# The slot table's rows by one indirect DMA of GpSimd per block, and the destination numbers behind the last product on DVE

## The chip, the cores and the metric

One core of a Trainium2 chip runs the whole program. The metric is the time of one execution on the device in microseconds (us), as the median of several runs. PE is TensorE, DVE is VectorE, ACT is ScalarE, POOL is GpSimd and SP is SyncE; SP and ACT can issue hardware DMAs, GpSimd issues DMAs whose descriptors software makes.

## The reference

The kernel computes two layers of a hybrid block over 512 latent tokens and 256 context tokens of 1024 features. In each layer come an adaptive layer norm, one input projection for three parallel mixers (short convolution, windowed attention, chunkwise mLSTM), their merge, and then a mixture of experts in two steps: the best of 4 groups, and in it the best 2 of 8 experts. Only the last concerns the change:

```python
def _hier_moe(h, w_rg, b_rg, w_re, b_re, w_ei, w_eo):
    ...
    g_sel = jnp.argmax(g_logit, axis=-1).astype(jnp.int32)
    ...
    top_l, top_i = lax.top_k(e_logit, TOP_K)
    wts = (jax.nn.softmax(top_l, axis=-1) * g_prob[rows, g_sel][:, None]).reshape(A)
    eid = (g_sel[:, None] * EXPERTS_PER_GROUP + top_i).reshape(A)
    ...
    def expert_block(args):
        xblk, e = args
        gt, up = jnp.split(xblk @ w_ei[e], 2, axis=-1)
        return (jax.nn.silu(gt) * up) @ w_eo[e]
    ...
    out = jax.ops.segment_sum(yb * buf_w[:, None], buf_tok, num_segments=N + 1)
```

An expert's `w_ei` is 1024x1024, its `w_eo` 512x1024, both f32.

## The kernel before, in words

`moe` (from L1186) does the experts of one layer. The weights of the 32 experts are streamed once per layer in 384 chunks of 128x1024 f32, 512 KB each: 8 of `w_ei` and 4 of `w_eo` per expert. SP issues one DMA per chunk (`Chunks.load`, L1223, into the tiles `er`; the tiles `wr`, `wh` and `wl`, which the dense products use too, by `wload`, L300). The chunks go around a ring of 40 tiles and, late in the layer, of 32; `fill` issues them as far as the ring goes, in the order of use that `order` gives.

Which expert comes when is decided at run time: the first NFIX (4) experts are fixed, the others are ranked by their number of tokens (`ranks`, from L1456), so that the k-th place in the program has blocks of a size that suits the k-th rank (`BLOCKS`: one, two or three blocks of 128, 64 or 32 rows). `eid`, a row of 32 integers, holds the expert of every place. SP and ACT read their registers from it.

The slot table `tbl` lies in DRAM, a row of four 32-bit words for each slot of each expert: token, destination row, weight, and one unused. `slots_of(e)` (from L1432) loads the rows of each block of place e into a tile `ib` of 128x4, out of 16 buffers. A block of 128 rows is one ACT DMA; a smaller one repeats itself down the 128 partitions and takes four ACT DMAs of 32x4. The address needs the expert's number, which ACT reads into a register. There are 84 such blocks in both layers, 8 of 128 rows and 76 smaller ones.

One pass of the main loop (from L1500) does expert e: `slots_of(e + 4)`; `fill`; `gather_of(e + 2)`, in which GpSimd gathers the tokens' rows into one of two tiles `xg` (L1268, an indirect DMA by column 0 of `ib`); the last products of `up`; `hidden`, in which PE's sums become `z` or `sg`, are transposed by PE and go through silu (ACT) and a product (DVE) into `g`; `down`, the second product; and `deliver`: ACT scales the sums by column 2 of `ib` into `ys` (L1370), and GpSimd scatters `ys` into `yd` (L1380, an indirect DMA). For blocks under 128 rows the destination rows come from `to`, which DVE computes from column 1 of `ib` (L1372, 128x1, four buffers). Between the halves of `hidden`, PE does the first products of expert e + 1, whose rows it has transposed into `x` (L1320, L1322). `z` is copied by ACT for blocks of 64 rows and by DVE for blocks of 32 (L1353).

Each engine works through its instructions in the order in which the scheduler put them. Every hardware DMA of SP or ACT gets one of eight completion semaphores (DMAHW0 to 7), in turn over both engines, and waits for the one before it on the same semaphore; those of GpSimd use eight others (DMASW0 to 7) in the same way.

Of the kernel before, what the change touches and what calls it, by code (L numbers as in the profile page):

```python
# [12 lines left out]
I32 = mybir.dt.int32  # L13
# [7 lines left out]
DEPTH = 2  # L21
# [7 lines left out]
NE = 32  # L29
# [60 lines left out]
def shape_consts():  # L90
    p = np.arange(128)[:, None]
    j = np.arange(128)[None, :]
    ident = (p == j).astype(np.float32)
    neg = np.float32(-BIG)
    m_prev = np.where(j >= p, 0, neg).astype(np.float32)
    m_next = np.where(j <= p, 0, neg).astype(np.float32)
    l_f = np.where(p <= j, 0, BIG).astype(np.float32)
    l_b = np.where(p >= j, 0, BIG).astype(np.float32)
    tri = 32.0 * (p < j).astype(np.float32)
    ones = np.ones((128, 128), np.float32)  # L100
    pos = np.arange(NL)
    nf = 16
    inv = (np.float32(10000.0) ** (-np.arange(nf, dtype=np.float32) / np.float32(nf))).astype(np.float32)
    cos = np.zeros((128, NL), np.float32)
    sin = np.zeros((128, NL), np.float32)
    for q in range(128):
        d = q % 64
        ps = (pos // 64 if d < 32 else pos % 64).astype(np.float32)
        ang = (ps * inv[d % 16]).astype(np.float32)
        cos[q] = np.cos(ang)  # L110
        sin[q] = np.sin(ang) * (-1.0 if d % 32 < 16 else 1.0)
    rst = np.ones((128, NL), np.float32)
    rst[:32, 0::128] = 0
    rst[32:, 127::128] = 0
    iota = np.broadcast_to(np.arange(32), (128, 32))
    lvl, lvl2 = (np.broadcast_to(np.arange(6) * v, (128, 6)) for v in (4096, 8))
    pidx = np.arange(128)[:, None]
    part = np.concatenate([pidx // 64, pidx // 32], 1)
    tie = np.broadcast_to(np.where(np.arange(32) < NFIX, -1e5 * (1 + np.arange(32)), 0) + 31 - np.arange(32), (128, 32))
    srank = np.broadcast_to(np.array(SRANK).reshape(1, -1), (128, 32 * DEPTH))  # L120
    caps = np.broadcast_to(np.array([sum(b) for bl in BLOCKS for b in bl])[None], (128, 32 * DEPTH))
    slot0 = np.broadcast_to(32 * np.arange(128)[None], (128, 128))
    parts = [("ident", ident), ("mp", m_prev), ("mn", m_next), ("lf", l_f), ("lb", l_b),
             ("tri", tri), ("ones", ones), ("iota", iota), ("lvl", lvl), ("lvl2", lvl2), ("pidx", pidx), ("part", part),
             ("tie", tie), ("srank", srank), ("caps", caps), ("slot0", slot0)]
    def cat(ps):
        off, o = {}, 0
        for n, a in ps:
            off[n] = (o, a.shape[1])
            o += a.shape[1]  # L130
        return off, np.ascontiguousarray(np.concatenate([a for _, a in ps], 1).astype(np.float32))
    rope = np.concatenate([cos, sin], 1)
    co, ca = cat(parts)
    tok = np.zeros((DEPTH, 128, 6, 2, 4), np.int32)
    for l in range(DEPTH):
        for t in range(6):
            for jj in range(2):
                tok[l, :, t, jj, 0] = t * 128 + np.arange(128)
                tok[l, :, t, jj, 1] = jj * NTOK[l] + t * 128 + np.arange(128)
    return co, ca, rst, rope, tok  # L140
# [80 lines left out]
def _build(nc, tc, I, OUT, es, dbg, stop):  # L221
# [964 lines left out]
    def moe(L, last, st_m, st_r, ahead):  # L1186
# [5 lines left out]
        comb = None  # L1192
        wei, weo = I["w_ei"][l * NE:(l + 1) * NE], I["w_eo"][l * NE:(l + 1) * NE]
        t128 = tbl[l][0:lv * 4096, :].rearrange("(n p e) c -> n p e c", p=128, e=32)
        t16, t32 = (tbl[l][0:lv * 4096 + 3584 // k * k].rearrange("(n p e) c -> n p e c", p=p, e=32)
                    for p, k in ((16, 512), (32, 1024)))
        st_m.close()
        with L.st_e as st_e:
            E1 = pool(st_e, "moe1")
# [137 lines left out]
            def hidden(M, ps):  # L1337

                gt_ = E.tile([128, 4, M], F32, name=f"g{M}", tag=f"g{M}", bufs=1 if M == 128 else 2)
                g = gt_.rearrange("p k m -> p (k m)")  # L1340
                if M == 128:
                    sg = E.tile([128, 512], F32, name="sg", tag="z64", bufs=1)
                    S.activation(sg, ps[:, 0:512], AF.Silu)
                    V.tensor_mul(sg, sg, ps[:, 512:1024])
                    yield
                    T = ps_t()
                    for k in range(4):
                        P.transpose(T[:, k * 128:(k + 1) * 128], sg[:, k * 128:(k + 1) * 128], ident)
                    S.copy(g, T)
                    yield gt_  # L1350
                    return
                z = E.tile([128, 8 * M], F32, name="z", tag=f"z{M}", bufs=1)
                (S.copy if M == 64 else V.tensor_copy)(z, ps[:, 0:8 * M])  # L1353
                yield
                T, n, nq = ps_t(), M // 16, 128 // M
                for k in range(n):
                    P.transpose(T[:, k * 128:(k + 1) * 128], z[:, k * 128:(k + 1) * 128], ident)  # L1357
                T = T[:, 0:8 * M].rearrange("p (k q m) -> p k q m", q=nq, m=M)
                gq = g.rearrange("p (q k m) -> p k q m", k=n, m=M)
                S.activation(gq, T[:, :, 0:nq // 2, :], AF.Silu)  # L1360
                V.tensor_mul(gq, gq, T[:, :, nq // 2:nq, :])
                yield gt_

            def deliver(M, idx, y, dyn):

                wt = idx[:, 2:3].bitcast(F32)
                if M < 128:
                    nq = 128 // M
                    ys = E.tile([128, 8 * M], F32, name="ys", tag=f"ys{M}", bufs=1)
                    S.activation(ys, y[:, 0:8 * M], AF.Copy, scale=wt)  # L1370
                    to = E.tile([128, 1], I32, name="to", tag="to", bufs=4)
                    V.tensor_scalar(to, idx[:, 1:2], float(nq), con("part")[:, nq // 4:nq // 4 + 1], ALU.mult, ALU.add)  # L1372
                    dst, top = yd[l].rearrange("n (q c) -> (n q) c", q=nq), 2 * nq * N - 1
                else:
                    ys = E.tile([128, DM], F32, name="ys", tag="ys", bufs=1)
                    for hf in range(2):
                        c = slice(hf * 512, (hf + 1) * 512)
                        S.activation(ys[:, c], y[hf], AF.Copy, scale=wt)
                    to, dst, top = idx[:, 1:2], yd[l][:, :], 2 * N - 1
# [11 lines left out]
            class Expert:  # L1391
# [17 lines left out]
                def hidden(self):  # L1409
                    h = [hidden(M, p) for M, p in zip(self.M, self.ps)]  # L1410
                    for g in h:
                        next(g)
                    yield
                    self.a = [next(g) for g in h]
                    yield

                def down(self, dyn=None):
# [9 lines left out]
                        for k, w in enumerate(ws):  # L1427
                            product(p if M == 128 else outs(M, p), x, k, w, k == 0, k == 3)
                    for i, (M, p) in enumerate(zip(self.M, y)):
                        deliver(M, dyn if dyn is not None else slots[self.e][i][1], p, dyn is not None)  # L1430

            def slots_of(e):  # L1432
                if e >= NE:
                    return
                if e < NFIX:
                    ev = slice(e, e + 1)
                else:
                    ev = ds(S.value_load(eid[0:1, e:e + 1], min_val=0, max_val=NE - 1), 1)
                slots[e], at = [], 0
                for M in BLOCKS[l][e]:  # L1440
                    ib = E.tile([128, 4], I32, name="ib", tag="ib", bufs=16)
                    if M == 128:
                        S.dma_start(ib, t128[at // 128][:, ev, :])
                    else:
                        for p in range(0, 128, 32):
                            S.dma_start(ib[p:p + 32, :], t32[(at + p % M) // 32][:, ev, :])
                    at += M
                    slots[e].append((M, ib))

            cnt, key = E.tile([128, 32], F32, name="cnt"), E.tile([128, 32], F32, name="key")  # L1450
# [1 line left out]
            rank, capc = E.tile([32, 1], F32, name="rank"), E.tile([32, 1], F32, name="capc")  # L1452
            place, cap = E.tile([32, 32], F32, name="place"), E.tile([128, 32], F32, name="cap")
            eid = E.tile([1, 32], I32, name="eid")

            def ranks():  # L1456

# [11 lines left out]
                V.tensor_scalar(place, con("srank")[0:32, 32 * l:32 * l + 32], rank, None, ALU.is_equal)  # L1469
                yield  # L1470
                T = ps_t()
                P.matmul(T[0:1, 0:32], con("pidx")[0:32, :], place, start=True, stop=True)
                V.tensor_copy(eid, T[0:1, 0:32])
                V.tensor_mul(cmp, place, con("caps")[0:32, 32 * l:32 * l + 32])
                V.tensor_reduce(capc, cmp, axis=X_AXIS, op=ALU.add)
                yield
# [9 lines left out]
                    cur.up(ks)  # L1486
                next(steps, None)
            fill(wc.n + EARLY)
            slots_of(2)
            slots_of(0)  # L1490
            slots_of(1)
            slots_of(3)
            for e in range(NE):
                slots_of(e + 4)
                used = wc.n - len(wc.raw)
                fill(min(used + RING + NX, max(used, LONG * (RING + NX)) + RING))
                nxt = Expert(e + 1, blocks[e + 1]) if e + 1 < NE else None
# [273 lines left out]
```

## Time and profile before

| | |
|---|---|
| median of 3 runs | 2537.89 us (2536.97 to 2543.22) |
| the profiled execution | 2534.49 us |
| its span | 2532.7 us |
| mean granted clock of PE | 0.936 |
| busy: PE, DVE, ACT, POOL | 89%, 39%, 29%, 12% |
| expert loop of layer 0 | about 784 to 1373 us |
| expert loop of layer 1 | about 1932 to 2494 us |

In a row of the windows stand the stretch and its length, then for PE, PEld (PE's weight load), DVE, ACT and POOL the busy time with the number of instructions, then the granted clock (1.00 is 2.4 GHz), the share of the DMA engines' time and what they moved in GB/s. In a row of the waits stand the engine and the line, what it waited for, the sum in us, how many waits and the longest; SPq and ACTq are the queues from which SP and ACT issue DMAs. In a row of the timeline stand start and duration in us, engine, line, what is done, and in brackets the idle time before with what ended it. In the page's groups the count is followed by busy time and mean ns of one, then the idle time before with its largest cause. What an engine does off the path costs nothing.

### The profile page before, as it was taken

To read this page: it belongs to the slowest core of one execution; us is meant where nothing else is said; L and a number is where in the kernel's file an instruction comes from. 1 tells how busy PE (TensorE), PEld (TensorE's weight loads), DVE (VectorE), ACT (ScalarE), POOL (GpSimd) and SP (SyncE) were. 2 spreads that over 40 slices of the span, in tenths; PEclk is the share of its full clock that TensorE was granted. 3 is DMA by queue.
4 is the path that set the end of the run, shared out by engine and by line. 5 is a ranking of instruction groups with operands and counts; after the bars stand their busy time and mean duration, and the time that the engine had idled before them with its cause. 6 is when DMAs were issued, how large, how long until landed. Compare 5 with 4: busy or idle time off the path is not lost. (4 is left out here: it accounts for less than half of the span.)

```text
span 2532.7 us, 40175 instructions
## 1 busy us (share of the span) xinstructions
PE 2253.1 (89%) x14591; PEld 1367.2 (54%) x14591; DVE 995.7 (39%) x2238; ACT 742.7 (29%) x1310; POOL 295.3 (12%) x289
## 2 busy tenths in 40 slices
PE   7999999999996999998986799999995998797874
PEld 4889777778873333333422577778873333232221
DVE  5686766684662000000101885775573000010003
ACT  3655444424421111111111754434431111111111
POOL 0000110010031211111101220000022111111101
PEclk9999999999997999998978899999997998898886
DMA  8878643457668998999995621235658888999996
GB/s 335 291 259 262 229 136 127 142 190 249 222 227 286 334 340 324 331 334 349 403 392 229 249 77 59 75 122 184 220 200 290 318 304 298 347 346 400 391 409 237
DMA packets 223455, 666.07 MB, mean 263 GB/s; under 512 B 46501, under 2 KB 57201, under 8 KB 223254
## 3 DMA queue, kind: packets, MB, share of 16 engines
q1 hardware_dynamic: 181238, 617.92, 67.2%
q10 hardware_dynamic: 29280, 24.50, 2.9%
q0 software_dynamic: 12736, 21.06, 2.6%
q8 instruction: 116, 1.90, 0.3%
q14 instruction: 85, 0.70, 0.1%
HBM read 629.38 MB, written 51.77 MB: 269 GB/s over the span
## 5 line engine op out<-in xcount | busy, mean ns | idle before, releaser
L1329 PE MATMUL pss<-er,x 128*32 128x256 f32 (+2 forms) x2592 | 439.4, 514 | 10.9 <-DMA er<-in_w_ei_dram 6.8
L345 PE MATMUL mm<-hh,wh 128*128 128x512 f32 (+1 forms) x1136 | 413.6, 365 | 5.5 <-DVE arow L363 3.6
L346 PE MATMUL mm<-hl,wh 128*128 128x512 f32 (+1 forms) x1136 | 408.5, 360 | 0.8 <-DVE hl L307 0.8
L347 PE MATMUL mm<-hh,wl 128*128 128x512 f32 (+1 forms) x1136 | 406.3, 358 | 3.1 <-DVE wl L307 2.0
L1372 DVE TENSOR_SCALAR to<-ib,ca 128x1 int32<-128x1 int32 x76 | 16.2, 214 | 766.8 <-DMA yd<-ys,to 587.0
L1329 PEld LDWEIGHTS pss<-er,x 128*32 128x32 f32 (+2 forms) x2592 | 142.1, 132 | 248.5 <-issue 175.5
L307 DVE TENSOR_TENSOR wl<-wr,wh 128x1024 fp32r<-128x1024 f32 x180 | 220.3, 1225 | 134.4 <-ACT wh L306 132.6
L306 ACT CAST wh<-wr 128x1024 fp32r<-128x1024 f32 x180 | 188.5, 1047 | 269.3 <-PE mm L346 200.6
L345 PEld LDWEIGHTS mm<-hh,wh 128*128 128x128 f32 x1136 | 215.0, 189 | 47.5 <-issue 11.7
L347 PEld LDWEIGHTS mm<-hh,wl 128*128 128x128 f32 x1136 | 215.2, 190 | 34.5 <-DVE wl L307 3.8
L346 PEld LDWEIGHTS mm<-hl,wh 128*128 128x128 f32 x1136 | 215.4, 190 | 30.6 <-issue 2.6
L1329 PE MATMUL mm<-er,g 128*32 128x256 f32 (+2 forms) x1192 | 189.4, 497 | 8.2 <-DMA er<-in_w_eo_dram 8.0
L1370 ACT ACTIVATE ys<-mm,ib 128x512 f32<-128x512 f32 (+1 forms) x71 | 41.2, 588 | 415.1 <-PE mm L1329 370.0
L1380 POOL DMA_INDIRECT yd<-ys,to x76 | 76.0, 1000 | 513.4 <-ACT ys L1370 461.7
L1329 PEld LDWEIGHTS mm<-er,g 128*32 128x32 f32 (+2 forms) x1192 | 62.0, 128 | 130.5 <-issue 89.7
L1268 POOL DMA_INDIRECT xg<-h2d,ib x76 | 72.7, 957 | 395.8 <-PE pst L1320 337.9
L1357 PE MATMUL pst<-ca,z 128*128 128x128 f32 x232 | 44.8, 304 | 70.8 <-DVE z L1353 55.8
L1329 PE MATMUL pss<-wr,x 128*32 128x256 f32 (+2 forms) x728 | 93.3, 458 | 10.5 <-ACT x L1322 5.5
L1320 PEld LDWEIGHTS pst<-ca,xg 64*128 64x128 f32 (+2 forms) x672 | 56.0, 152 | 61.1 <-issue 43.5
L1357 PEld LDWEIGHTS pst<-ca,z 128*128 128x128 f32 x232 | 25.6, 147 | 115.6 <-issue 54.7
L1320 PE MATMUL pst<-ca,xg 64*128 64x64 f32 (+2 forms) x672 | 68.4, 246 | 18.4 <-DMA xg<-h2d,tb 17.4
L763 POOL TENSOR_TENSOR ke<-mk,ct 128x256 f32<-128x256 f32 x24 | 17.4, 754 | 527.6 <-ACT wh L306 187.2
(396 smaller groups left out, 3100.2 us busy)
## 6 DMA issues: line engine op xcount, KB each, us to landing
er<-in_w_ei_dram SPq DMA_DIRECT2D x348, 512.0 KB
er<-in_w_eo_dram SPq DMA_DIRECT2D x174, 512.0 KB
wr<-in_w_in_dram SPq DMA_DIRECT2D x142, 512.0 KB
wr<-in_w_ada_dram SPq DMA_DIRECT2D x96, 512.0 KB
wr<-in_w_ei_dram SPq DMA_DIRECT2D x84, 512.0 KB
wl<-in_w_ei_dram SPq DMA_DIRECT2D x42, 512.0 KB
wr<-in_w_eo_dram SPq DMA_DIRECT2D x42, 512.0 KB
wh<-in_w_ei_dram SPq DMA_DIRECT2D x38, 512.0 KB
```

The lines of the kernel that those rows point to most:

```text
L306: S.copy(hi, t)
L307: (eng or V).tensor_sub(lo, t, hi.bitcast(F32))
L345: P.matmul(out, ah, bh, start=first, stop=False)
L346: P.matmul(out, ah, bl, start=False, stop=False)
L347: P.matmul(out, al, bh, start=False, stop=last)
L763: G.tensor_mul(ke[i, d], mk[:, j].rearrange("p (a b c) -> p b a c", a=2, b=2), ct[:, j, 6 + d, :].rearrange("p (b a) -> p b a", b=2).unsqu ...
L1268: ins = G.indirect_dma_start(x[at:at + R, :], None, h2d[l][:, :], bass.IndirectOffsetOnAxis(ap=idx[0:R, 0:1], axis=0), bounds_check=N - 1, ...
L1320: P.transpose(T[:, j * M:(j + 1) * M], x[at:at + M, k * 128:(k + 1) * 128], ident[at:at + M, at:at + M])
L1329: P.matmul(o, x[:, k, :], w[:, q * n:(q + 1) * n], start=first, stop=last)
L1357: P.transpose(T[:, k * 128:(k + 1) * 128], z[:, k * 128:(k + 1) * 128], ident)
L1370: S.activation(ys, y[:, 0:8 * M], AF.Copy, scale=wt)
L1380: st = G.indirect_dma_start(dst, bass.IndirectOffsetOnAxis(ap=to, axis=0), ys, None, bounds_check=top, oob_is_err=False)
```

## The change

The constants get a column block `pat` per layer: for each place and each of its up to three blocks, 32 times the slot of partition p. `ranks` computes the expert numbers on all 128 partitions (one product that broadcasts `pidx`) and one DVE instruction adds `pat`: `srow`, 128x32x3 row numbers of the table. `slots_of` becomes one indirect DMA of GpSimd per block, 128 rows of 16 bytes; ACT issues no `ib` and reads no registers any more. And `to` is placed behind the last product of its own expert on DVE (`issue_after(pin)`, where `hidden` hands back the instruction of that product).

```diff
@@ shape_consts
+    pat = np.zeros((DEPTH, 128, NE, 3))
+    for l in range(DEPTH):
+        for e, bl in enumerate(BLOCKS[l]):
+            for i, m in enumerate(bl):
+                pat[l, :, e, i] = 32 * (sum(bl[:i]) + np.arange(128) % m)
...
+    parts += [(f"pat{l}", pat[l].reshape(128, 96)) for l in range(DEPTH)]
@@ hidden
-                V.tensor_mul(gq, gq, T[:, :, nq // 2:nq, :])
-                yield gt_
+                yield gt_, V.tensor_mul(gq, gq, T[:, :, nq // 2:nq, :]).ins
@@ deliver
-                    V.tensor_scalar(to, idx[:, 1:2], float(nq), con("part")[:, nq // 4:nq // 4 + 1], ALU.mult, ALU.add)
+                    with tc.issue_after(pin):
+                        V.tensor_scalar(to, idx[:, 1:2], float(nq), con("part")[:, nq // 4:nq // 4 + 1], ALU.mult,
+                                        ALU.add)
@@ Expert.hidden
-                    self.a = [next(g) for g in h]
+                    a = [next(g) for g in h]
+                    self.a, self.pin = [x for x, _ in a], a[-1][1]
@@ slots_of
-                if e < NFIX:
-                    ev = slice(e, e + 1)
-                else:
-                    ev = ds(S.value_load(eid[0:1, e:e + 1], min_val=0, max_val=NE - 1), 1)
-                slots[e], at = [], 0
-                for M in BLOCKS[l][e]:
+                slots[e] = []
+                for i, M in enumerate(BLOCKS[l][e]):
                     ib = E.tile([128, 4], I32, name="ib", tag="ib", bufs=16)
-                    if M == 128:
-                        S.dma_start(ib, t128[at // 128][:, ev, :])
-                    else:
-                        for p in range(0, 128, 32):
-                            S.dma_start(ib[p:p + 32, :], t32[(at + p % M) // 32][:, ev, :])
-                    at += M
+                    G.indirect_dma_start(ib, None, tbl[l][:, :], bass.IndirectOffsetOnAxis(ap=srow[:, e, i:i + 1], axis=0),
+                                         bounds_check=lv * 4096 - 1, oob_is_err=False)
@@ ranks
-                P.matmul(T[0:1, 0:32], con("pidx")[0:32, :], place, start=True, stop=True)
+                P.matmul(T[:, 0:32], con("pidx")[0:32, :].to_broadcast([32, 128]), place, start=True, stop=True)
                 V.tensor_copy(eid, T[0:1, 0:32])
+                V.tensor_tensor(srow, T[:, 0:32].unsqueeze(2).to_broadcast([128, 32, 3]),
+                                con(f"pat{l}").rearrange("p (e b) -> p e b", b=3), ALU.add)
```

Three places of the order show what moves. First SP, in layer 0 where the loop has begun and the first `eid` is read: the weight DMAs with their waits, as they stood before (`er` and `wr` are weight tiles, DMAHW the completion semaphores).

```order
L1223 DMA er0_8252<-in_w_eo_dram 128x1024 [waits DMAHW7_49,PE_49]
L1223 DMA er1_8254<-in_w_ei_dram 128x1024 [waits DMAHW3_49,PE_49]
L1223 DMA er2_8256<-in_w_ei_dram 128x1024 [waits DMAHW7_49,PE_49]
L1223 DMA er3_8258<-in_w_ei_dram 128x1024 [waits DMAHW3_49,PE_49]
L1244 TENSOR_LOAD eid_8175 [waits DVE_49]
L1244 ISA x2
L1223 ISA
L1223 DMA er4_8269<-in_w_ei_dram 128x1024 [waits DMAHW7_49,PE_49]
L300 ISA
L300 DMA wr_8474<-in_w_ei_dram 128x1024 [waits DMAHW3_49,PE_49]
```

The same place of SP after the change.

```order
L1229 DMA er0_8254<-in_w_eo_dram 128x1024 [waits DMAHW2_49,PE_49]
L1229 DMA er1_8256<-in_w_ei_dram 128x1024 [waits DMAHW3_49,PE_49]
L1229 DMA er2_8258<-in_w_ei_dram 128x1024 [waits DMAHW4_49,PE_49]
L1229 DMA er3_8260<-in_w_ei_dram 128x1024 [waits DMAHW5_49,PE_49]
L1250 TENSOR_LOAD eid_8175 [waits DVE_49]
L1250 ISA x2
L1229 ISA
L1229 DMA er4_8271<-in_w_ei_dram 128x1024 [waits DMAHW6_49,PE_49]
L307 ISA
L307 DMA wr_8448<-in_w_ei_dram 128x1024 [waits DMAHW7_49,PE_49]
```

Before, consecutive weights wait on DMAHW7 and DMAHW3 by turns; after, on all eight in turn.

Then DVE, just behind, from the end of `ranks` on, as it was before (`z` and `g64`, `g32` are steps of `hidden` for a block of 64 and one of 32 rows).

```order
L1372 TENSOR_SCALAR to_8637<-ib_8296,ca_68 128x1 [waits DMAHW2_49,DMAHW6_49,DMAHW1_49,DMAHW0_49]
L1353 COPY z_8375<-pss_8207 128x256 [waits Activation_49]
L1361 TENSOR_TENSOR g64_8371<-g64_8371,pst_8390 128x256 [waits Activation_49]
L1361 TENSOR_TENSOR g32_8374<-g32_8374,pst_8397 128x2x2x32 [waits Activation_49]
L1372 TENSOR_SCALAR to_8811<-ib_8271,ca_68 128x1 [waits DMASW2_49]
L1372 TENSOR_SCALAR to_8818<-ib_8276,ca_68 128x1 [waits DMASW3_49]
L1353 COPY z_8557<-pss_8377 128x256 [waits DVE_49,Activation_49]
```

DVE from the end of `ranks` on after the change.

```order
L1359 COPY z_8359<-pss_8208 128x256 [waits Activation_49]
L1367 TENSOR_TENSOR g64_8355<-g64_8355,pst_8374 128x256 [waits Activation_49]
L1367 TENSOR_TENSOR g32_8358<-g32_8358,pst_8381 128x2x2x32 [waits Activation_49]
L1378 TENSOR_SCALAR to_8432<-ib_8281,ca_68 128x1 [waits DMASW0_49]
L1378 TENSOR_SCALAR to_8439<-ib_8285,ca_68 128x1 [waits DMASW1_49]
L1359 COPY z_8531<-pss_8361 128x256 [waits DVE_49,Activation_49]
L1367 TENSOR_TENSOR g64_8527<-g64_8527,pst_8546 128x256 [waits Activation_49]
```

Before, the two `to` between one expert's `g` and the next `z` wait on DMASW, for scatters; after, the `to` there wait on DMASW0 and DMASW1, which belong to the `ib` that they read, and one `to` has gone from ahead of the first `z`.

Last POOL, from the first scatters of layer 0 on (`yd` is the scatter, `xg` the gather), before.

```order
L1380 DMA yd0_91<-ys_8446,to_8448 3072x512 [waits DMASW2_49,DVE_49,Activation_49]
L1380 DMA yd0_91<-ys_8453,to_8455 6144x256 [waits DMASW3_49,DVE_49,Activation_49]
L1268 DMA xg1_7987<-h2d0_89,ib_8320 64x1024 [waits DMAHW0_49,DMAHW6_49,DMASW6_49,PE_49]
L1380 DMA yd0_91<-ys_8628,to_8630 3072x512 [waits DVE_49,Activation_49]
L1268 DMA xg0_7986<-h2d0_89,ib_8469 64x1024 [waits DMAHW5_49,DMAHW6_49,DMASW0_49,PE_49]
L1380 DMA yd0_91<-ys_8635,to_8637 6144x256 [waits DMASW7_49,DVE_49,Activation_49]
L1268 DMA xg0_7986<-h2d0_89,ib_9479 32x1024 [waits DMAHW5_49,DMASW1_49,PE_49]
```

POOL from its first scatters on after the change.

```order
L1387 DMA yd0_91<-ys_8430,to_8432 3072x512 [waits DMASW2_49,DVE_49,Activation_49]
L1445 DMA ib_9290<-tbl0_93,srow_8176 128x4 [waits DMASW3_49]
L1387 DMA yd0_91<-ys_8437,to_8439 6144x256 [waits DMASW4_49,DVE_49,Activation_49]
L1274 DMA xg1_7987<-h2d0_89,ib_8305 64x1024 [waits DMASW5_49,PE_49]
L1445 DMA ib_9384<-tbl0_93,srow_8176 128x4 [waits DMASW6_49]
L1387 DMA yd0_91<-ys_8602,to_8604 3072x512 [waits DMASW7_49,DVE_49,Activation_49]
L1445 DMA ib_9388<-tbl0_93,srow_8176 128x4 [waits DMASW0_49]
L1387 DMA yd0_91<-ys_8609,to_8611 6144x256 [waits DMASW1_49,DVE_49,Activation_49]
L1274 DMA xg0_7986<-h2d0_89,ib_8444 64x1024 [waits DMASW2_49,PE_49]
```

Before, scatters and gathers follow one another; after, an `ib` of a later expert stands between most of them.

## Rows read from the trace of the kernel before

**Rows 1.** Windows: busy time by engine, granted clock, DMA share, GB/s.

```profile
784.00:870.00 86.00, 77.06 (x643) 31.09 (x643) 7.59 (x35) 12.90 (x27) 14.63 (x15) 0.93 0.89 298
870.00:1160.00 290.00, 275.67 (x1523) 108.26 (x1522) 17.37 (x49) 42.32 (x83) 42.26 (x43) 0.97 0.91 336
1160.00:1350.00 190.00, 174.78 (x1163) 62.67 (x1163) 13.88 (x45) 28.75 (x55) 24.26 (x25) 0.92 0.99 382
1314.00:1330.00 16.00, 16.00 (x90) 5.18 (x94) 0.29 (x1) 1.88 (x3) 0.95 (x1) 0.66 0.97 377
1932.00:2020.00 88.00, 76.77 (x653) 31.43 (x657) 7.81 (x33) 12.68 (x28) 12.98 (x14) 0.94 0.85 290
2020.00:2300.00 280.00, 242.47 (x1478) 93.45 (x1477) 17.65 (x57) 36.34 (x72) 38.20 (x39) 0.93 0.91 331
2300.00:2480.00 180.00, 140.76 (x1034) 48.69 (x1022) 8.39 (x29) 21.27 (x42) 19.59 (x20) 0.83 1.02 400
```

**Rows 2.** Waits of SP, 2020 to 2300: line, cause, sum, times, longest.

```profile
SPq L1223 <- DMA ib<-tbl: 39.0, 15, 9.7
SPq L300 <- DMA ib<-tbl: 29.4, 10, 6.5
...
SPq L1223 <- PE pss L1329: 5.7, 19, 0.4
```

**Rows 3.** Timeline 2126 to 2140: start, duration, instruction, idle before in brackets.

```profile
2127.21 11.73 SPq L1223 DMA_DIRECT2D er<-in_w_ei_dram  x4
...
2133.43 4.97 ACTq L1446 DMA_DIRECT2D ib<-tbl  x8
```

**Rows 4.** DMA view, 2020 to 2300: ACT's queue, packets, MB, share.

```profile
q10 hardware_dynamic: 3216, 0.04, 0.7%
```

**Rows 5.** The page's groups: `to`.

```profile
L1372 DVE TENSOR_SCALAR to<-ib,ca 128x1 int32<-128x1 int32 x76 | 16.2, 214 | 766.8 <-DMA yd<-ys,to 587.0
```

**Rows 6.** Timeline 1313 to 1315, DVE and PE.

```profile
1313.31 0.21 DVE L1372 TENSOR_SCALAR to<-ib,ca 128x1 int32<-128x1 int32 x1 [0.35 <-DMA yd<-ys,to]
1313.44 0.41 DVE L1353 COPY z<-pss 128x256 f32<-128x256 f32 x1
1314.00 0.66 PE L1357 MATMUL pst<-ca,z 128*128 128x128 f32 x2 [6.73 <-DVE z L1353]
```

**Rows 7.** Waits of PE, 784 to 1373.

```profile
PE pst L1357 <- DVE z L1353: 13.0, 7, 6.7
...
PE pst L1357 <- ACT z L1353: 6.6, 7, 2.4
PE pst L1348 <- DVE sg L1344: 5.5, 2, 2.8
PE pst L1460 <- ACT x L1322: 3.6, 1, 3.6
PE pss L1329 <- DVE sg L1344: 3.1, 2, 2.8
```

**Rows 8.** Timeline 806 to 812, ACT.

```profile
809.03 0.86 ACT L1322 COPY x<-pst 128x512 f32<-128x512 f32 x2 [18.57 <-DMA ib<-tbl]
```

**Rows 9.** Waits of SP, 2300 to 2490, the largest.

```profile
SPq L1223 <- DMA er<-in_w_ei_dram: 25.3, 32, 2.0
```

**Rows 10.** Waits of PE, 1932 to 2020.

```profile
PE pss L1329 <- ACT x L1322: 3.5, 1, 3.5
PE pst L1357 <- DVE z L1353: 3.2, 2, 2.5
```

**Rows 11.** Timeline 786 to 790, POOL.

```profile
787.96 0.91 POOL L1268 DMA_INDIRECT xg<-h2d,ib  x1 [0.31 <-issue]
```

**Rows 12.** The page's groups: `yd` and `xg`.

```profile
L1380 POOL DMA_INDIRECT yd<-ys,to x76 | 76.0, 1000 | 513.4 <-ACT ys L1370 461.7
...
L1268 POOL DMA_INDIRECT xg<-h2d,ib x76 | 72.7, 957 | 395.8 <-PE pst L1320 337.9
```

**Rows 13.** Tile `xg`, 2030 to 2120.

```profile
DMA to landing us min/median/max: 6.7/7.2/7.6
```

More of the change, by code (lines that the diff above doesn't have):

```diff
@@ L1194, in moe @@
         t128 = tbl[l][0:lv * 4096, :].rearrange("(n p e) c -> n p e c", p=128, e=32)
-        t16, t32 = (tbl[l][0:lv * 4096 + 3584 // k * k].rearrange("(n p e) c -> n p e c", p=p, e=32)
-                    for p, k in ((16, 512), (32, 1024)))
+        t16 = tbl[l][0:lv * 4096 + 3584].rearrange("(n p e) c -> n p e c", p=16, e=32)
         st_m.close()
@@ L1349, in hidden @@
                     S.copy(g, T)
-                    yield gt_
+                    yield gt_, None
                     return
@@ L1360, in hidden, with deliver @@
                 S.activation(gq, T[:, :, 0:nq // 2, :], AF.Silu)
-                V.tensor_mul(gq, gq, T[:, :, nq // 2:nq, :])
-                yield gt_
-            def deliver(M, idx, y, dyn):
+                yield gt_, V.tensor_mul(gq, gq, T[:, :, nq // 2:nq, :]).ins
+            def deliver(M, idx, y, dyn, pin):
                 wt = idx[:, 2:3].bitcast(F32)
@@ L1429, in down @@
                     for i, (M, p) in enumerate(zip(self.M, y)):
-                        deliver(M, dyn if dyn is not None else slots[self.e][i][1], p, dyn is not None)
+                        deliver(M, dyn if dyn is not None else slots[self.e][i][1], p, dyn is not None, self.pin)
             def slots_of(e):
-                if e >= NE:
-                    return
-                if e < NFIX:
-                    ev = slice(e, e + 1)
-                else:
-                    ev = ds(S.value_load(eid[0:1, e:e + 1], min_val=0, max_val=NE - 1), 1)
-                slots[e], at = [], 0
-                for M in BLOCKS[l][e]:
-                    ib = E.tile([128, 4], I32, name="ib", tag="ib", bufs=16)
-                    if M == 128:
-                        S.dma_start(ib, t128[at // 128][:, ev, :])
-                    else:
-                        for p in range(0, 128, 32):
-                            S.dma_start(ib[p:p + 32, :], t32[(at + p % M) // 32][:, ev, :])
-                    at += M
+                slots[e] = []
+                for i, M in enumerate(BLOCKS[l][e]):
+                    ib = E.tile([128, 4], I32, name="ib", tag="ib", bufs=16)
+                    G.indirect_dma_start(ib, None, tbl[l][:, :], bass.IndirectOffsetOnAxis(ap=srow[:, e, i:i + 1], axis=0),
+                                         bounds_check=lv * 4096 - 1, oob_is_err=False)
                     slots[e].append((M, ib))
@@ L1454, in moe @@
             eid = E.tile([1, 32], I32, name="eid")
+            srow = E.tile([128, 32, 3], I32, name="srow")
             def ranks():
@@ L1488, in moe @@
             fill(wc.n + EARLY)
[L1489 to L1492, printed above, removed]
+            for e in (2, 0, 1, 3):
+                slots_of(e)
             for e in range(NE):
-                slots_of(e + 4)
+                if e + 4 < NE:
+                    slots_of(e + 4)
                 used = wc.n - len(wc.raw)
```

## The prediction

> **What bounds the kernel now.** First the windows, cut at the stages of the two expert loops [rows 1]. In layer 0 (784 to 1350, and some 20 us more) PE is busy 90%, 95% and 92% of the three stretches: it sets the pace. In layer 1 that holds until 2020 at most; in 2300 to 2480 PE's share is down to 78% while the DMA share stands at 1.02 and 400 GB/s: there the weights set the pace. Between them, 2020 to 2300 is the odd stretch: the DMA engines move only 331 GB/s, hardly other than in 870 to 1160 (336), and the weights fall behind.
>
> Why they move so little stands in SP's waits of that stretch [rows 2]: SP, which issues the weights, waits 39.0 and 29.4 us for `ib` transfers, which no weight needs, and only 5.7 for PE to leave a tile of the ring. It waits because the transfers of SP and of ACT take turns on the same eight completion semaphores (in the first order excerpt above the `er` alternate between two names; the rest have gone to `ib`). What that looks like [rows 3]: four weight issues take 11.73 us from 2127.21, until eight `ib` issues on ACT have ended at 2138.4. The traffic of ACT's own queue is no cause: 3216 packets, 0.7% of the DMA engines' time [rows 4].
>
> The second loss is on DVE. `to`, 214 ns of work, has 766.8 us of idle time ahead of it, 587.0 of them for a scatter [rows 5]. DVE is idle often, so that alone is harmless; but at 1313.31 a `to` that a scatter has just released stands ahead of the copy `z` of 1313.44, and PE starts at 1314.00, after 6.73 us [rows 6]. The waits of PE in layer 0 name `z` and `sg` on DVE (13.0, 5.5, 3.1) and `z` and `x` on ACT (6.6, 3.6), 31.8 us together [rows 7]. Behind PE's 6.73 us the granted clock of 1314 to 1330 is 0.66 with PE busy throughout [rows 1]: part of that stretch ran at 1.2 GHz instead of 2.4, so a wait is paid a second time. ACT's share shows at the start of the loop: a copy `x` comes after 18.57 us in which ACT waited and issued for `ib` [rows 8].
>
> **The change, part by part.** The sum is made against the profiled execution, 2534.5 us; the median of the runs is 3.4 above it.
>
> *Layer 1's weights.* 304 small transfers and 8 larger ones leave ACT, and with them their turns on the eight semaphores; in the order SP now has them alone, 2, 3, 4, 5, 6, 7. A weight then waits for the weight eight before it, as SP's waits name weights first in 2300 to 2490 already [rows 9], where the rate is 400 GB/s [rows 1]. At this rate the bytes of 2020 to 2300 take 280 x 331/400 = 232 us: **-48**. The near end is 0 (rate unchanged), the far end the two waits themselves, 39.0 + 29.4 = 68. I take the rate, because it is measured on the same queue with the same tiles. PE does not stand against it: 242.5 us busy at a clock of 0.93 are 225 at the full one.
>
> *The start of layer 1.* From 1932 to 2020 PE is busy 87% and the weights move at 290 GB/s, so PE leads; it waits 3.5 us for `x` and 3.2 for `z` [rows 10], both behind `ib` or `to`: **-5**, between 0 and -7.
>
> *Layer 0.* PE sets the pace, so its waits are worth their length: of 31.8 us I take 27, since some of ACT's `z` (7 waits) are the copy's own time. The lower clock costs (1-0.93) x 86 + (1-0.97) x 290 + (1-0.92) x 190 = 30 us against full speed [rows 1]; not every drop follows one of these waits, so 18 of it: **-45** together, between -20 (half the waits, a little clock) and -62 (all of both). Would the weights keep up? 298 x 86, 336 x 290 and 382 x 190 are 196 MB, 489 us at 400 GB/s; the 566 us of these stretches shortened by 45 are 521. That is closer than before, a reason not to take the far end. The DVE chain that ranks the experts loses its four `to` as well, which is in this sum.
>
> *What it costs.* GpSimd issues 84 transfers more. An indirect one holds it 0.91 us and follows the one before after 0.31 [rows 11]; with the 0.957 of `xg` [rows 12] that is 1.27 each, 107 us over both loops. GpSimd's `yd` and `xg` had 461.7 us of waiting for `ys` and 337.9 for PE, so I put the time into these waits: 0 on the path; without that cover, part of the 107 would come back (the second rival). Between a `yd` and the next `xg` mostly one `ib` stands (third excerpt). The first gathers of each layer are an exception: nine `ib` now go ahead of them, 9 x 1.27 = 11.4 us, and an `ib` takes about as long to land as an `xg`, 7.2 us [rows 13], all behind `srow`. In layer 0 they used to be issued near 787.96, an expert or more ahead of need: I take 1 us late per layer, between 0 and 5. `srow` is one DVE instruction of 96 elements, nearest to the 0.21 of `to` [rows 6], in a chain freed of four of them: +0.2 a layer. The constants are 98 KB larger, 0.25 us at 400 GB/s. `to` is moved, not added; it now waits for an `ib` that landed long before and for the scatter of four blocks ago. PE's product for 128 rows instead of one stays one instruction. Together **+3**, between +1 and +15.
>
> Sum: -48 - 5 - 45 + 3 = **-95**, so 2439.5 in a profile and **2443** as a median. All ends together are unlikely; some two thirds of the way to them gives 2409 to 2486 for this case.
>
> **Rivals.** *The weights are not freed.* The 16-byte rows have still to be moved, through the same DMA engines; if the 331 GB/s came from them, only waits go: half of layer 0's 31.8 us (its weights would then lag), 5 of clock and the 5 of layer 1's start, -26, so 2512. Against it: 0.7% of the engines' time [rows 4], and SP's waits that name `ib` [rows 2]. The Trainium skill, "DMA: Bandwidth & Descriptors", section "Issuing engines are not separate DMA queues", speaks for this rival: transfers of all issuers run on the same 16 engines, and another issuer saves only the sequencer's time for issuing. By that rule the first term would be 0 and the time 2512; the trace shows shared semaphores besides, of which that section says nothing. I give it 0.09.
>
> *GpSimd's gathers come late.* `xg` has two buffers, so a gather goes out when PE has turned the rows of an expert before, and lands 7.2 us later [rows 13]; an expert of 32 rows is short, and an `ib` ahead costs 1.27. If half of the 76 gathers lay bare, 38 x 1.27 = 48 us come back: 2491. Against it: the 337.9 us in which `xg` waited for PE [rows 12], time in which an `ib` has already gone. 0.10.
>
> *Slower: a landing in front of the gathers.* GpSimd's transfers take turns on eight semaphores of their own, so each waits for the one eight before, and with an `ib` in every round that one is nearer in time. Where it hasn't landed, GpSimd stands still with `yd` and `xg` behind it, and an expert loses up to a landing of 7.2 us. For half of the 56 experts whose number is found at run time that is 28 x 7.2 = 202 us: 2443 + 202 = 2645. It decides where eight issues take less than a landing. Back to back they take 8 x 1.27 = 10.2 us against 7.6 at most [rows 13], so at this load it does not; with longer landings it would. 0.05.
>
> *Nothing.* The terms cancel to within what a measurement can tell here, 0.3% or 8 us: 0.02.
>
> **How the numbers follow.** The forecast has 0.74, the rivals 0.09, 0.10 and 0.05, the rest 0.02. Faster is the forecast with the first two rivals, 0.93; same 0.02; slower 0.05. The range starts at 2400, just under the far ends of all terms, 2537.9 - 68 - 7 - 62 + 1 = 2402, and goes to 2498, which takes in the late gathers and leaves out the unfreed weights and the slower case.
>
> **What would show it.** Right: no `ib` among SP's waits; the counterpart of 2020 to 2300 at 390 GB/s or more, with PE waiting for weights almost from its beginning; no `to` with a scatter ahead of it; PE's waits for `z`, `sg` and `x` in layer 0 down to some 5 us and its clock there at 0.96 or more; GpSimd busy some 80 us longer and idle for PE and `ys` by as much less. The first step is wrong if the rate stays near 335 though the `ib` waits are gone; layer 0's, if weights bind it before it is 45 us shorter; the cost, if PE waits for `xg` of run-time experts. The forecast as a whole is wrong above 2490.

## The result and the profile after

| | before | after |
|---|---|---|
| median | 2539.18 us (2536.97 to 2543.22, 4 runs) | 2476.74 us (2475.35 to 2481.93, 4 runs) |
| ratio | | 0.9756, 95% interval 0.9736 to 0.9776 |
| span of the profiled execution | 2532.7 us | 2473.3 us |
| mean granted clock | 0.936 | 0.946 |
| GpSimd busy | 295.3 us | 381.9 us |

The kernel became faster by 62 us where 95 were forecast. First the windows of the changed kernel, cut at its own stages (its loops run from about 784 to 1348 and from 1900 to 2435).

```profile
784.00:870.00 86.00, 73.00 (x557) 28.97 (x561) 6.58 (x31) 10.44 (x22) 31.84 (x32) 0.87 0.72 252
870.00:1000.00 130.00, 129.34 (x750) 53.02 (x747) 7.91 (x23) 21.61 (x42) 32.26 (x33) 1.00 1.02 386
1000.00:1150.00 150.00, 146.73 (x862) 56.70 (x859) 8.90 (x27) 23.08 (x45) 36.84 (x37) 1.00 1.03 397
1150.00:1320.00 170.00, 165.71 (x1157) 61.47 (x1155) 13.72 (x47) 27.69 (x54) 25.60 (x26) 0.96 0.96 362
1900.00:1990.00 90.00, 71.02 (x535) 27.97 (x535) 6.29 (x28) 10.60 (x22) 31.84 (x33) 0.84 0.67 236
1990.00:2100.00 110.00, 107.03 (x761) 43.98 (x758) 7.27 (x24) 17.50 (x36) 29.14 (x29) 0.98 1.02 386
2100.00:2260.00 160.00, 149.79 (x998) 58.50 (x997) 12.48 (x41) 23.40 (x46) 33.83 (x34) 1.00 1.03 394
2260.00:2420.00 160.00, 125.60 (x866) 37.00 (x864) 7.21 (x26) 18.75 (x37) 17.70 (x18) 0.84 1.01 396
```

Two things stand in these rows. From 870 to 1150 and from 1990 on the weights move at 386 to 397 GB/s, where [rows 1] had 336 and 331, and PE's clock is 0.96 to 1.00 until the last stretch, in which it waits some 28 us for weights. But the first window of each loop is worse than before: 252 GB/s at a clock of 0.87 where [rows 1] had 298 and 0.93 (layer 0), 236 GB/s at 0.84 where it had 290 and 0.94 (layer 1).

SP's waits in 1990 to 2260, the stretch that answers to [rows 2], name no `ib` at all; they are waits for earlier weights.

```profile
SPq L1229 <- DMA er<-in_w_ei_dram: 39.9, 47, 2.0
SPq L1229 <- DMA er<-in_w_eo_dram: 20.4, 22, 1.8
...
SPq L1229 <- PE pss L1335: 7.7, 19, 1.5
```

PE's waits in the expert loop of layer 0, which answer to [rows 7]:

```profile
PE pst L1326 <- DMA xg<-h2d,tb: 11.6, 1, 11.6
PE pst L1363 <- issue: 9.3, 5, 5.7
PE pss L1335 <- issue: 4.9, 6, 0.9
PE pst L1363 <- ACT z L1359: 4.0, 6, 0.7
PE pst L1363 <- DVE z L1359: 1.0, 3, 0.5
PE pst L1354 <- DVE sg L1350: 0.9, 1, 0.9
```

`z` and `sg` are down to 4.0 + 1.0 + 0.9 = 5.9 us. In their place stand waits that the profile puts down to nothing ("issue"), 9.3 and 4.9 us; for the gather by `tb`, the row numbers of the first two experts, PE waits 11.6 (8.3 before). Last the page's groups of GpSimd, of which the first two answer to [rows 12]:

```profile
L1387 POOL DMA_INDIRECT yd<-ys,to x76 | 77.0, 1013 | 420.3 <-ACT ys L1375 395.4
...
L1274 POOL DMA_INDIRECT xg<-h2d,ib x76 | 72.6, 955 | 273.9 <-PE pst L1326 235.8
...
L1445 POOL DMA_INDIRECT ib<-tbl,srow x84 | 85.3, 1016 | 75.9 <-DMA yd<-ys,ib 33.9
```

84 transfers of 1.0 us went into GpSimd's waits for `ys` and for PE, which fell by 66 and 102 us. A new wait of GpSimd stands in front of `ib`, for the landing of an earlier scatter:

```profile
POOL ib L1445 <- DMA yd<-ys,ib: 33.9, 6, 7.9
```

To see where in a loop time is won or lost, the scatters `yd` serve as milestones: there are 45 in layer 0 and 39 in layer 1, in the same order in every version. The table has their starts, from the timelines of the profiled executions; the first row of each timeline stands below it.

| us | first of layer 0 | last of layer 0 | first of layer 1 | last of layer 1 |
|---|---|---|---|---|
| before | 823.8 | 1377.4 | 1970.9 | 2494.1 |
| after | 833.6 | 1348.9 | 1957.4 | 2435.4 |
| difference | +9.8 | -28.5 | -13.5 | -58.7 |

Before:

```profile
823.80 1.02 POOL L1380 DMA_INDIRECT yd<-ys,to  x1 [15.55 <-ACT ys L1370]
```

After:

```profile
833.57 1.02 POOL L1387 DMA_INDIRECT yd<-ys,to  x1 [10.38 <-ACT ys L1375]
```

Each timeline is one execution, and that of before lies at the low end of its times: the medians of before, measured beside each group of the experiments below, are 2543.4 to 2548.1 us. A gain over before at the last milestone reads 4 to 16 us smaller than the gain by the medians in every version here; differences between two other versions do not depend on it.

So the loops themselves won 38.3 us in layer 0 (from +9.8 to -28.5) and 45.2 in layer 1 (from -13.5 to -58.7). The start of each loop, up to the first scatter, lost: the first gather of the loop stood 1.1 us earlier than before, so layer 0 lost 10.8 there, and layer 1, counted from the last scatter of layer 0, lost 15.0. What happens in such a start shows on PE from 806 to 824 (timeline of PE, after):

```profile
807.53 0.59 PE L1335 MATMUL pss<-wr,x 128*32 128x256 f32 x3 [0.79 <-issue]
808.95 0.63 PE L1335 MATMUL pss<-wr,x 128*32 128x256 f32 x4 [0.83 <-issue]
810.40 0.61 PE L1335 MATMUL pss<-wr,x 128*32 128x256 f32 x1 [0.83 <-issue]
816.73 1.54 PE L1363 MATMUL pst<-ca,z 128*128 128x128 f32 x6 [5.72 <-issue]
...
820.98 0.59 PE L1335 MATMUL pss<-wr,x 128*64 128x512 f32 x1 [0.85 <-issue]
822.38 0.59 PE L1335 MATMUL pss<-er,x 128*64 128x512 f32 x1 [0.81 <-issue]
```

A weight load and a matmul come every 1.40 us, with nothing named that they wait for. It is not PE alone. The tile view of `wr` has SP's register moves in 800 to 836, three of them, with the least, median and largest duration in ns:

```profile
L307 SPq MOVE wr<-in_w_ei_dram x3: 688/700/703, 806.8 to 817.4; - x3
```

Some 0.70 us for a move of a register; in the kernel before it is 29 to 38 ns throughout the loops. Four weights take SP 20.16 us to issue (timeline of SP):

```profile
806.13 20.16 SPq L307 DMA_DIRECT2D wr<-in_w_ei_dram  x4
```

ACT is late too: between the table load at 816.70 and the silu behind it, it is idle for 8.14 us, against 1.54 in the version `both` below. In this stretch GpSimd issues a series of 20 indirect DMAs back to back, one every 1.3 us, from 797.56 to 823.2: nine `ib`, four gathers and seven more `ib`.

### The profile page after: what moved, and what is told of

Read it like the earlier page. It is cut to its first block, busy times and chain, and to the rows that moved or that the text cites. A ratio compares the mean times of both kernels' runs of the same rounds, so it can differ in the third digit from the quotient of the medians.

```text
span 2473.3 us, 39181 instructions
## 1 busy us (share of the span) xinstructions
PE 2236.8 (90%) x14591; PEld 1361.1 (55%) x14591; DVE 994.1 (40%) x2240; ACT 742.4 (30%) x1310; POOL 381.9 (15%) x373
## 4 chain that ended last, share of the span: by engine, by line
PE 66%; DMA 15%; DVE 7%; issue 6%; POOL 2%; ACT 2%; another core or an unknown queue 1%; SPq 0%; POOLq 0%; ACTq 0%; DVEq 0%
PE pss L1335 19%; PE mm L1335 9%; PE mm L352 7%; PE mm L353 7%; PE mm L354 7%; DMA er<-in_w_ei_dram 5%; DMA er<-in_w_eo_dram 3%; PE pst L1326 2%; PE pss L643 2%; PE pst L653 1%; PE pst L1363 1%; POOL lsm L429 1%; PE mm L367 1%; DVE wl L314 1%
## 5 line engine op out<-in xcount | busy, mean ns | idle before, releaser
L1335 PE MATMUL pss<-er,x 128*32 128x256 f32 (+2 forms) x2592 | 433.3, 501 | 14.3 <-DMA er<-in_w_ei_dram 12.4
L1359 DVE COPY z<-pss 128x256 f32<-128x256 f32 x36 | 15.3, 424 | 471.9 <-PE pss L1335 222.3
L1335 PE MATMUL mm<-er,g 128*32 128x256 f32 (+2 forms) x1192 | 183.6, 488 | 10.0 <-DMA er<-in_w_eo_dram 9.8
L1367 DVE TENSOR_TENSOR g<-g,pst 128x256 f32<-128x256 f32 (+1 forms) x76 | 25.9, 356 | 340.3 <-ACT g L1366 302.0
L1335 PE MATMUL pss<-wr,x 128*32 128x256 f32 (+2 forms) x728 | 102.9, 468 | 12.1 <-issue 8.3
L1445 POOL DMA_INDIRECT ib<-tbl,srow x84 | 85.3, 1016 | 75.9 <-DMA yd<-ys,ib 33.9
L1326 PE MATMUL pst<-ca,xg 64*128 64x64 f32 (+2 forms) x672 | 64.3, 237 | 23.1 <-DMA xg<-h2d,tb 22.4
```

Of the source, the lines that this page charges most:

```text
L1326: P.transpose(T[:, j * M:(j + 1) * M], x[at:at + M, k * 128:(k + 1) * 128], ident[at:at + M, at:at + M])
L1335: P.matmul(o, x[:, k, :], w[:, q * n:(q + 1) * n], start=first, stop=last)
L1445: G.indirect_dma_start(ib, None, tbl[l][:, :], bass.IndirectOffsetOnAxis(ap=srow[:, e, i:i + 1], axis=0), bounds_check=lv * 4096 - 1, oob_ ...
```

## The experiments

Theory S: the series is what slows the start, because in it the instructions of the other engines come at some 0.7 us each. Theory G, the rival that the prediction had in its sum: the first gathers come late, behind nine `ib`. Beside them the question which of the change's two parts brought what.

**The parts alone.** `pin_only` is the kernel before with `to` placed behind its expert's product (and `pin` handed down to it, as in the change) and nothing else:

```diff
-                    V.tensor_scalar(to, idx[:, 1:2], float(nq), con("part")[:, nq // 4:nq // 4 + 1], ALU.mult, ALU.add)
+                    with tc.issue_after(pin):
+                        V.tensor_scalar(to, idx[:, 1:2], float(nq), con("part")[:, nq // 4:nq // 4 + 1], ALU.mult,
+                                        ALU.add)
```

> The kernel before with only the destination numbers placed behind the last product; the table rows still come by ACT's DMAs. If the two parts work as the prediction says, only the DVE stalls go: layer 0 some 15 to 25 us shorter, layer 1 hardly (its weights still wait for ib), 2512 to 2525. If the whole gain comes from ACT and the semaphores: 2535 to 2540.

Measured: 2506.95 us, 0.9859 of before (0.9825 to 0.9894), a gain somewhat larger than expected. Its milestones are +0.2, -19.6, -16.9, -29.4: layer 0 gained 20 us and layer 1, from its first scatter on, 12.5. SP's waits in 1990 to 2260 still name `ib`, and the window of that stretch still has 344 GB/s:

```profile
SPq L1223 <- DMA ib<-tbl: 28.5, 8, 6.1
...
SPq L300 <- DMA ib<-tbl: 25.2, 12, 6.6
```

```profile
1990.00:2260.00 270.00, 237.43 (x1518) 91.57 (x1518) 17.73 (x58) 37.04 (x74) 40.27 (x41) 0.96 0.94 344
```

`no_pin` is the changed kernel with the same lines the other way round (the indentation and `issue_after` taken out).

> The changed kernel without the placing of the destination numbers. If the placing is worth what the DVE waits of before said: 10 to 20 us slower than the change, 2487 to 2497, with PE waiting for z behind a number that waits for a scatter. If the move of the table rows to GpSimd alone does it all: 2475 to 2480.

Measured: 2548.25 us against 2548.1 of before on the same chip, 1.0005 (0.9992 to 1.0018). Both expectations missed: without the placing the move of the table rows brings nothing on balance. The milestones (+15.7, +20.0, +36.3, +12.1) show what is in the balance: each start loses some 16 us, layer 0 then loses 4 more, and layer 1 wins 24 from its first scatter on. The weights were free (2100 to 2260 at 397 GB/s), but `to` waited for scatters longer than in [rows 5], 725.6 us, and PE for `z` (1932 to 2300). Window, DVE's wait and PE's waits:

```profile
2100.00:2260.00 160.00, 133.43 (x833) 53.86 (x833) 8.79 (x26) 21.56 (x42) 31.91 (x32) 0.91 1.03 397
```

```profile
DVE to L1377 <- DMA yd<-ys,to: 725.6, 63, 25.2
```

```profile
PE pst L1363 <- DVE z L1359: 21.4, 5, 7.6
PE pst L1363 <- ACT z L1359: 13.2, 6, 8.5
```

**The start.** `fixed_act` loads the rows of the four fixed experts, whose place in the table is known, by six DMAs of ACT ahead of the ranking:

```diff
+            fx = E.tile([128, 2, NFIX, 4], I32, name="fx")
+            t32 = tbl[l][0:96 * 32, :].rearrange("(p e) c -> p e c", e=32)
+            for i, M in enumerate(FIXED):
+                for p in range(0, 128, M):
+                    S.dma_start(fx[p:p + M, i, :, :], t32[sum(FIXED[:i]):sum(FIXED[:i]) + M, 0:NFIX, :])
...
             def slots_of(e):
+                if e < NFIX:
+                    slots[e] = [(M, fx[:, i, e, :]) for i, M in enumerate(FIXED)]
+                    return
```

> The changed kernel, but the table rows of the four fixed experts come by six DMAs of ACT before the ranking, so the gathers of experts 2 and 3 need not wait for GpSimd's nine. GpSimd still issues some 13 table-row DMAs back to back right behind them. Theory S (a long series of GpSimd DMAs slows every engine's instructions, 0.7 us each): the loss of 11 to 15 us at the start of each loop stays, 2470 to 2480. Theory G (the first gathers come late): the loss goes, 2445 to 2455.

Measured: 2473.33 us, 0.9706 (0.9685 to 0.9726), milestones +12.2, -28.5, -15.3, -60.2. GpSimd's timeline shows the gather of expert 2 at 788.60 and that of expert 3 at 802.34, ahead of most of the series, and yet the first scatter is no earlier than with the change:

```profile
788.60 0.95 POOL L1274 DMA_INDIRECT xg<-h2d,fx  x1 [0.30 <-PE pst L1326]
...
802.34 0.95 POOL L1274 DMA_INDIRECT xg<-h2d,fx  x1 [0.30 <-issue]
...
836.05 1.02 POOL L1387 DMA_INDIRECT yd<-ys,to  x1 [14.53 <-ACT ys L1375]
```

The gathers are no longer late, PE's waits in the loop of layer 0 name no gather but the one by `tb` (8.8 us), and the loss is still there: G falls, as S said. `both` adds that a later block's rows are issued behind the gather before them, so that they come one or two at a time:

```diff
-                if e + 4 < NE:
-                    slots_of(e + 4)
...
                 gather_of(e + 2)
+                if e + 4 < NE:
+                    with tc.issue_after(gathers[-1]):
+                        slots_of(e + 4)
```

> As fixed_act, and each later block's table rows are issued behind the gather of the expert two places earlier, so that no series of GpSimd DMAs is left at the start of a loop. Theory S: the slow stretch at the start of each loop goes (no register move of SP over 0.1 us there, PE without gaps between its instructions), 2448 to 2458. Theory G alone gives the same as fixed_act. If the start is slow for another reason: 2470 to 2480.

Measured: 2432.36 us, 0.9542 (0.952 to 0.9565), 16 us below the range that S gave; milestones -7.8, -49.6, -55.3, -99.6. The first scatter of layer 0, the window of the 20 us of the start, and SP's register moves (four of them) in `both`:

```profile
816.04 1.03 POOL L1387 DMA_INDIRECT yd<-ys,to  x1 [13.42 <-ACT ys L1375]
```

```profile
798.00:818.00 20.00, 20.00 (x184) 8.78 (x183) 1.85 (x8) 4.62 (x9) 3.92 (x4) 1.00 0.95 348
```

```profile
L307 SPq MOVE wr<-in_w_ei_dram x4: 29/29/29, 798.5 to 806.0; - x4
```

The same 20 us of the start in the changed kernel:

```profile
806.00:826.00 20.00, 9.36 (x33) 3.33 (x33) 0.43 (x1) 1.87 (x2) 13.23 (x14) 0.68 0.33 100
```

184 matmuls against 33, at a granted clock of 1.00 against 0.68: PE stands idle for 5.72 us from 811.0 on, and the clock of 812 to 820 is 0.50, the level of 1.2 GHz. `spread` is the second step without the first (all rows by GpSimd, the later ones behind gathers):

> The changed kernel, all table rows by GpSimd, with the later blocks' rows behind the gathers as in both. Eight table-row DMAs still stand in a row at the start, some 14 GpSimd DMAs in all. Theory S (a long series slows every engine): the slow stretch is shorter than the change's 20 in a row, ratio to before 0.960 to 0.968, between both (0.954) and fixed_act (0.971). Theory G (first gathers late): like the change, 0.975.

Measured: 2471.92 us, 0.9719 (0.9699 to 0.9738), milestones +10.4, -26.4, -20.1, -64.3. This missed the expectation of S: against `both` its start costs 17 us in layer 0, counted from the loop's first gather, and 12 in layer 1, so a series of 14 indirect DMAs costs most of what one of 20 does (19 and 21, below). By its ratio `spread` cannot be told from the change (0.9731 below), which is what G expected; against G stand `fixed_act` and PE's waits in `spread`, which in layer 0 name no gather but that by `tb`. Neither step by itself is worth more than some 10 us; together they are worth 45.

**The cost by itself.** `junk` adds to `both` a number of table-row DMAs of GpSimd that nothing reads, behind the gathers of expert 2 (`ib` has 10 buffers instead of 16, to make room):

```diff
                 gather_of(e + 2)
...
+                if e == 0:
+                    jk = E.tile([128, 12, 4], I32, name="jk")
+                    for j in range(12):
+                        with tc.issue_after(gathers[-1]):
+                            G.indirect_dma_start(jk[:, j, :], None, tbl[l][:, :], bass.IndirectOffsetOnAxis(ap=srow[:, 4 + j, 0:1], axis=0),
+                                                 bounds_check=lv * 4096 - 1, oob_is_err=False)
```

> As both, with 12 more table-row DMAs of GpSimd per layer behind the gathers of expert 2, into a tile that nothing reads: the work left is the same, 12 indirect DMAs are added. Theory S: the slow stretch returns, PE at one matmul per 1.4 us while the series runs, SP's register moves at 0.7 us, 15 to 20 us per layer, ratio 0.966 to 0.970. Without S, GpSimd's own 15 us are covered as elsewhere: 0.954 to 0.957, and PE waits for a gather at most.

Measured: 2469.08 us, 0.9696 (0.9674 to 0.9718), milestones +11.2, -24.9, -15.9, -59.7. PE's waits in 796 to 836, and SP's register moves in 790 to 836:

```profile
PE pss L1335 <- issue: 5.1, 6, 1.5
```

```profile
L307 SPq MOVE wr<-in_w_ei_dram x4: 3/260/702, 800.6 to 822.4; - x4
```

Twelve transfers that nothing waits for cost 40 us, with the same marks as the change. That is S by itself. The transfers also keep the gather of expert 3 back (from 799.1 in `both` to 816.0), but PE's waits name no gather there; and the smaller number of `ib` buffers is not the cause, since `junk_plain` below has it too.

`junk5` has 5 of them.

> As junk with 5 instead of 12. Theory S with a cost in proportion to the series: 6 to 8 us per layer, ratio 0.959 to 0.961. Theory S with a beginning (the first 7 or so cost nothing, as in the trace of the change): 0 to 3 us per layer, ratio 0.954 to 0.957.

Measured: 2442.65 us, 0.9606 (0.9586 to 0.9626). By the ratios that is 16 us above `both`, by the medians, which are from different chips, 10; its profiled execution was only 2 us longer.

`junk_plain` has 12 plain DMAs of GpSimd in place of the 12 of `junk`, `G.dma_start(jk[:, j, :], t128[0][:, j, :])`, from fixed places of the table.

> As junk, but the 12 DMAs of GpSimd are plain ones of the same 128 rows of 16 bytes (fixed addresses, no index). If any DMA of GpSimd slows the engines in a series: like junk, 0.966 to 0.970. If it needs the indirect form: like both, 0.954 to 0.957.

Measured: 2434.39 us, 0.9568 (0.9547 to 0.959), milestones -8.6, -49.5, -55.6, -100.8: as `both`. SP's register moves in 790 to 836 of it:

```profile
L307 SPq MOVE wr<-in_w_ei_dram x4: 3/16/29, 797.6 to 805.3; - x4
```

The plain ones were not in quite the same place: they need no `srow`, take GpSimd 0.54 us each, and were done at 800.2, in groups of one to five with pauses between. So it is shown that a dozen DMAs of GpSimd need not cost anything; that the index makes the difference is likely, but not separated from the unbroken row and from the place.

**Once more, on one chip.**

> The changed kernel once more, as the measure for the three beside it on the same chip: ratio to before 0.974 to 0.977.

Measured: 2477.26 us, 0.9731 (0.9707 to 0.9755).

> The version without a series of GpSimd DMAs once more: 0.953 to 0.957, so 0.978 to 0.981 of the change beside it.

Measured: 2432.05 us, 0.955 (0.9526 to 0.9573): 45 us better than the change beside it. It beats both kernels.

> Five needless table-row DMAs per layer on the version without a series. Its trace showed 2 us lost at the start of layer 0 and none in layer 1, its ratio 16 us. If the trace is right (a series costs little up to about eleven): 0.000 to 0.002 above both_again. If the cost is in proportion: 0.006 above.

Measured: 2444.78 us, 0.9615 (0.9589 to 0.9641), 0.0065 above `both_again`: the proportional expectation. Its milestones are 3.2 us behind `both_again` at the first scatter and 7.5 at the last. So in this pair five cost 8 us (spans) to 13 (medians), in the pair before 2 to 16, and twelve 40. Whether there is a number below which a series is free stays open.

`both_nopin` is `both` without the placing of `to`.

> The version without a series, and without the placing of the destination numbers. If the placing is worth the same here as on the changed kernel (no_pin lost 0.025): 0.977 to 0.982. If no_pin lost only because the series delayed the scatters that the numbers wait for: 0.955 to 0.960.

Measured: 2492.28 us, 0.978 (0.9751 to 0.981): the placing is worth as much without the series as with it. Milestones -6.2, +0.4, -7.6, -40.9: layer 0 gains nothing that its milestones show without it, layer 1 still 33 us from its first scatter on, though PE waits there 55.6 us for `z` (PE's waits, 1900 to 2450):

```profile
PE pst L1363 <- DVE z L1359: 55.6, 15, 7.7
```

## Why the prediction was right, and where it missed

The direction held, and the time lies in the range, 34 us above the forecast. Step by step, by the milestones:

**Layer 1's weights, -48.** Measured -45.2 from the first scatter on. The rate came as forecast: no `ib` in SP's waits, 386 to 394 GB/s. `pin_only`, which kept ACT's DMAs, kept the `ib` waits and 344 GB/s, and `both_nopin`, which had the move without the placing, gained 33 there at 387 GB/s (1990 to 2260). So the size is in part luck: the sum put all of the 48 on the rate, but the move alone brought 33, and `pin_only` got 12.5 in this stretch from the placing, which the sum had not counted here. One sign failed too: PE was not waiting for weights almost from the beginning. In 1990 to 2260 it was busy 95% and waited 3.0 us for weights; with the weights freed PE set the pace there. The rival in which the weights are not freed is out. The Trainium skill, "DMA: Bandwidth & Descriptors", section "Issuing engines are not separate DMA queues", says that DMAs of every issuer run on the same 16 DMA engines, so that another issuer saves only the time of issuing. Here the rate rose all the same, from 331 to 394 GB/s: the issuing queue mattered through the shared completion semaphores.

**Layer 0, -45.** Measured -38.3 after the first scatter; in `both`, without the loss at the start, -41.8 after it. The 31.8 us of named waits are down to 5.9, and from 870 on the clock is 0.96 to 1.00. One thing the sum had wrong in kind: it treated the two parts as one sum of waits. The placing alone gave 20 us of it and the move alone none (`both_nopin`, +0.4): as soon as the table rows come from elsewhere the `to` left in front of `z` wait just as long for scatters, and only with both parts gone is the whole there.

**The start of layer 1, -5.** Measured +15.0; in `both` -5.7 (from -49.6 to -55.3). The step was right about the waits that went, and the loss came from elsewhere, the next point.

**What it costs, +3.** This is the step that failed. The prediction put GpSimd's 107 us at "0 on the path", since they lie in GpSimd's own waits, and gave the first gathers 1 us per layer. GpSimd's waits did take them. But the nine `ib` of each layer, with the seven behind them, form a series during which PE, SP and ACT get slower. Measured against `both`, which does the same work without a series, the start cost 18.9 us in layer 0 (+10.8 against -8.1, counted from the loop's first gather) and 20.7 in layer 1 (+15.0 against -5.7, counted from the last scatter of layer 0): 40 us in place of 3. Some 5 of these are not the series: for the first gather, by `tb`, PE waits 11.6 and 10.8 us in the two layers, in `both` 8.6 and 9.0, for a reason that no run shows. Late gathers behind the nine `ib` were not it (`fixed_act`). The rows read of before had no long series of indirect DMAs, so nothing stood behind the bound "+15" for one.

The other rivals: gathers of run-time experts were not waited for (PE's waits name only `tb`'s). Landings did stand in front of GpSimd's DMAs, though not in the way of the third rival: six `ib` waited 33.9 us together for the landing of a 128-row scatter that GpSimd had issued one to four DMAs earlier, not eight, and one gather 5.1 us for an `ib`. Since PE waited for no gather behind them, this cost nothing that PE's waits show. With the series taken out the sum is reached and passed: the span of `both` is 2432.9 us, 99.8 below that of before, and the medians taken side by side differ by 116 (`both`) and 111 (`both_again`), where the sum said 95.

One piece of the prediction's arithmetic does not come out: two thirds of the way from the forecast to all its ends is 2416 to 2503, not 2409 to 2486. The measured time lies in both.

## What to carry to other kernels

When hardware DMAs of a small, late kind share completion semaphores with a stream that must not stop, take them off that queue; and look for the instruction that waits in order behind them, because one repair without the other can be worth nothing where it is made (layer 0 gained 20 us by the placing alone, none by the move alone, 50 in the version `both`, which has the two). Work given to an idle engine is not free because that engine is idle: issue its indirect DMAs one or two at a time between other work, and load whatever has a known address by a plain DMA. A milestone that every version passes in the same order shows in which stretch a change gains and in which it gives back.

## What the runs showed of the hardware that was not expected

A series of some 14 to 20 indirect DMAs of GpSimd, one each 1.3 us, slowed the other engines of this kernel, which have nothing to do with it: from some 9 us after its first one PE got through 33 matmuls in 20 us (184 without it), at a mean granted clock of 0.68, a register move on SP took 0.70 us (29 ns without it), and four weights took SP 20.2 us to issue. Nine in a row (`junk5`) already left PE 2.0 us of waits put down to nothing. Why, no run settled. The DMA engines are not the reason: they had little to do. The DMA view of 804 to 826, changed kernel:

```profile
DMA packets 1072, 2.01 MB, mean 91 GB/s; under 512 B 588, under 2 KB 588, under 8 KB 1072
...
q1 hardware_dynamic: 432, 1.57, 21.2%
q0 software_dynamic: 640, 0.44, 9.2%
```

The same stretch of `both`:

```profile
DMA packets 2177, 7.20 MB, mean 327 GB/s; under 512 B 424, under 2 KB 424, under 8 KB 2175
...
q1 hardware_dynamic: 1868, 6.82, 88.8%
q0 software_dynamic: 307, 0.36, 5.8%
q8 instruction: 1, 0.02, 0.3%
q14 instruction: 1, 0.01, 0.1%
```

What the first lacks are the rows of the instruction queues (q8, q14): no block of instructions came in these 22 us. The Trainium skill, "Runtime: NRT & Kernel Launch", section "Instruction fetch mechanics", says that each sequencer fetches its program in blocks of 16 KiB through a DMA queue of its own, mostly unseen. A lack of instructions would fit. But `both` has no such row from 958 to 980 either, at 389 GB/s and full clock, so missing rows are no sign by themselves; a late block would make one long wait and not 0.70 us at each instruction, and fewer blocks are also what slow engines need. No run here tells cause from consequence.
